# One quarter row of a tile loaded in sixteen runs of partitions, and twenty load semaphores

## The chip, the core and the metric

The kernel runs on one core of one Trainium2 chip. Data lies in device memory and is brought into the core's on-chip memory of 128 partitions by loads that the queue of SyncE (SP) issues and that 16 DMA engines carry out. Three engines compute: ScalarE (ACT), GpSimd (POOL) and VectorE (DVE). TensorE is not used. The metric is the device time of one execution in microseconds (us).

## The reference

```python
batch, seq, dim = 32, 2048, 2048
x = np.random.randn(batch, seq, dim).astype(np.float32)
mask = np.random.rand(batch, seq, dim) < 0.1
x[mask] = np.nan
...
np.nanmax(x, axis=axis).astype(np.float32)
```

The last axis is reduced: 65,536 rows of 2,048 floats, 537 MB in all, each row to its largest value that is not NaN.

## The kernel before, in words

**Layout.** The 65,536 rows are dealt to the 128 partitions, 512 rows to each. The unit of the plan is a quarter row, 512 floats, 2 KB in each partition (`Q`, line 11). `TILES` (from line 16) lists 74 tiles; an entry is (loads, pieces, reds), all in quarter rows. Most tiles are of 28 quarter rows, seven whole rows in each partition, and are brought by one load of 128 partitions x 56 KB. The first tile is of 4 quarter rows, and in the tail the tiles are cut into more and smaller loads. `GROUPS` joins tiles whose rows lie together in device memory; the 30th tile is the last of the second group.

**Three steps in a tile.** The pieces say how much each cleaning step takes, the reds how much each maximum takes.
1. ACT (`e_key`, line 270's helper) reads the upper 16 bits of a piece in a tile buffer `xt` and writes a 16-bit key to a key buffer `kt`, in which a NaN becomes a value that turns into a very low number.
2. POOL turns the key back (times -1, plus a constant, line 280's helper) and writes it over the upper 16 bits in `xt`. For pieces with a negative number ACT does this instead.
3. DVE takes the maximum along each row from `xt` (`tensor_reduce`, line 287's helper) and writes it to `acc` or `lead`.

The usual tile of 28 has pieces 7, 9, 12 and reds 16, 12. Every eighth tile or so has 9, 12, -7 and 8, 20.

**Buffers.** There are three tile buffers (`BUFS`) and three key buffers. Tile n uses buffer n mod 3, so the load of tile n waits until DVE has done its last maximum of tile n - 3 (`free`, handed to `load` as `before`).

**Order and waits.** The class `Order` keeps, for each engine, the semaphore values that it has already seen, directly or through what another engine had seen. `add` puts an explicit wait in front of the instruction for every event that is still unseen except the last one, which the instruction itself waits for. A load is put on SP's queue by `load` (line 241). It uses one of `LANES` semaphores in turn, and waits for the load that used the same one before. All loads and the six stores go through SP's queue.

**Around the change.** In the loop `for loads, pieces, reds in g` (line 346) the counter `number` is 1 for the first tile after `number += 1`. The loop over `loads` (line 352) issues one load for each entry and notes in `landed` which columns of the tile it brings. A piece's ACT step waits for every entry of `landed` that overlaps its columns (`here`). The first three loads are issued ahead and taken from the list `ahead`.

## Time and profile before

| what | before |
|---|---|
| time, median of 3 runs | 1250.41 us (1250.36 to 1250.45) |
| span of the profiled execution | 1248.8 us |
| read from device memory | 536.87 MB, 430 GB/s over the span |
| loads of 7168 KB, issue to landing | 61, median 22.6 us |

The span runs from the first to the last instruction of one profiled execution; the time of a run lies 1.6 us above it here. In the profile a row of a group names the line, the engine, the operation, the tile written and the tile read, the shape, the count, the busy time and the mean, and after a bar the idle time of the engine before these instructions with what ended it. A row of the timeline gives start, duration, engine, line, operation and, in brackets, the idle time before it. A row of stretches gives the window, its length, and the busy time of DVE, ACT and POOL with their counts, then the TensorE clock, the DMA share and GB/s. The chain of waits is read from the last instruction back, each step to what released it. Many lines of the program are helpers, so L246 is every load, L270 every ACT step, L280 every POOL step, L287 every maximum.

### The profile page before, as it was taken

Reading aid. Unit: us, or ns where it says so; the run is one execution under the profiler, and the core shown is the slowest. Engines: PE = TensorE matmul, PEld = TensorE weight load, DVE = VectorE, ACT = ScalarE, POOL = GpSimd, SP = SyncE. Lnnn points to the kernel's source line nnn. Section 1 sums busy time; section 2 is a strip of 40 time slices with the busy share of each in tenths; the row PEclk is TensorE's granted clock in tenths of the full one; section 3 lists DMA queues with packets and bytes.
Section 4 is the critical chain, followed back from the end, with each engine's and each line's share of the span. In section 5 each row is a group of like instructions: output and inputs, shape, how many; then the busy total and the mean of one; then the engine's idle time right before and its main releaser. Section 6 shows DMA issues by size and latency. Waiting matters only on the chain.

```text
span 1248.8 us, 884 instructions
## 1 busy us (share of the span) xinstructions
DVE 1110.5 (89%) x181; ACT 968.8 (78%) x280; POOL 1164.9 (93%) x238
## 2 busy tenths in 40 slices
DVE  0888989888889888898988888988888989999999
ACT  3777887778777877788777877777777779989998
POOL 2999989998999899998999899999999999999998
DMA  9999999999999999999999999999999999999998
GB/s 416 441 413 439 441 441 425 428 441 441 428 425 441 441 435 417 441 441 439 426 428 441 439 432 422 441 441 435 419 439 441 435 430 432 429 432 427 431 428 326
DMA packets 16855, 537.20 MB, mean 430 GB/s; under 512 B 2640, under 2 KB 2640, under 8 KB 4944
## 3 DMA queue, kind: packets, MB, share of 16 engines
q1 hardware_dynamic: 16848, 537.14, 99.6%
q14 instruction: 7, 0.06, 0.0%
HBM read 536.87 MB, written 0.26 MB: 430 GB/s over the span
## 4 chain that ended last, share of the span: by engine, by line
DVE 38%; DMA 36%; POOL 17%; ACT 9%; issue 1%; SPq 0%
DMA xt<-in_x_dram 36%; DVE acc L287 22%; POOL xt L280 17%; DVE lead L287 16%; ACT kt L270 8%; ACT xt L270 1%; SPq L246 0%; SPq L264 0%; SPq L255 0%
## 5 line engine op out<-in xcount | busy, mean ns | idle before, releaser
L280 POOL TENSOR_SCALAR xt<-kt 128x6144 int16<-128x6144 uint16 (+9 forms) x232 | 1163.8, 5016 | 80.5 <-ACT kt L270 67.1
L270 ACT ACTIVATE kt<-xt 128x3584 uint16<-128x3584 int16 (+10 forms) x248 | 913.0, 3720 | 271.8 <-DMA xt<-in_x_dram 250.3
L287 DVE TENSOR_REDUCE acc<-xt 128x3 f32<-128x6144 f32 (+3 forms) x119 | 896.2, 7571 | 132.9 <-POOL xt L280 125.6
L287 DVE TENSOR_REDUCE lead<-xt 128x1 f32<-128x2048 f32 (+3 forms) x59 | 212.9, 3690 | 0.5 <-POOL xt L280 0.5
L270 ACT ACTIVATE xt<-kt 128x512 int16<-128x512 uint16 (+4 forms) x30 | 57.1, 1913 | 0.6
L270 ACT ACT_TABLE_LOAD x1 | 1.3, 1283 | 3.3 <-PEq L264 3.3
L319 DVE MEMSET lead<- 128x1 f32 x1 | 0.1, 59 | 3.4 <-PEq L264 3.4
L287 DVE SCALAR_TENSOR_TENSOR acc<-acc 128x414 f32<-128x414 f32 x1 | 1.2, 1178 | 0.0
L280 POOL TENSOR_SCALAR lead<-lead 128x91 int32<-128x91 f32 x1 | 0.6, 551 | 0.1
L315 POOL TENSOR_TENSOR lead<-lead 128x91 int32<-128x91 int32 x1 | 0.4, 376 | 0.1
L526 POOL MEMSET const-float32-0.0<- 128x1 f32 x1 | 0.1, 99 | 0.2 <-issue 0.2
L270 ACT ACTIVATE lead<-lead 128x1 f32<-128x1 f32 x1 | 0.2, 203 | 0.0
L287 DVE SCALAR_TENSOR_TENSOR lead<-lead 128x7 f32<-128x7 f32 x1 | 0.2, 168 | 0.0
L526 POOL MEMSET const-bfloat16-1.0<- 128x1 bf16 x1 | 0.1, 102 | 0.0
L526 POOL MEMSET const-uint8-127<- 128x1 uint8 x1 | 0.1, 102 | 0.0
L526 POOL MEMSET const-float32-1.0<- 128x1 f32 x1 | 0.1, 99 | 0.0
## 6 DMA issues: line engine op xcount, KB each, us to landing
xt<-in_x_dram SPq DMA_DIRECT2D x61, 7168.0 KB, 22.6
xt<-in_x_dram SPq DMA_DIRECT2D x3, 4096.0 KB, 18.6
xt<-in_x_dram SPq DMA_DIRECT2D x5, 2048.0 KB, 27.5
xt<-in_x_dram SPq DMA_DIRECT2D x3, 3072.0 KB, 25.5
xt<-in_x_dram SPq DMA_DIRECT2D x2, 4352.0 KB, 16.5
xt<-in_x_dram SPq DMA_DIRECT2D x3, 2816.0 KB, 23.3
xt<-in_x_dram SPq DMA_DIRECT2D x2, 3584.0 KB, 25.2
xt<-in_x_dram SPq DMA_DIRECT2D x5, 1024.0 KB, 27.6
```

What stands on the lines that cost most here:

```text
L270: lambda: nc.scalar.activation(**kw),
L280: lambda: nc.gpsimd.tensor_scalar(**kw),
L287: return order.add("dve", nc.vector, lambda: do(**kw), deps)
L315: lambda: nc.gpsimd.tensor_tensor(out=bits, in0=bits, in1=none, op=ALU.add),
L319: e_warm = order.add("dve", nc.vector, lambda: nc.vector.memset(warm, 1.0), [])
L526: nc = _bacc.Bacc("TRN2", target_bir_lowering=False, num_devices=1)
```

## The change

The 30th tile's entry gets two loads, of 27 quarter rows and of 1. The load of 27 is issued as any other. The one quarter row behind it (`at` is not 0) is issued as sixteen loads, each of the same 512 columns but of a run of neighbouring partitions: 15, 14, 13, ... 1 of them, and 8 twice, 128 in all. Each has an entry in `landed` with the same columns, so ACT's piece over these columns waits for all of them. The number of load semaphores goes from 14 to 20. Pieces and reds of the tile are the same.

```diff
-    + [([28], [7, 9, 12], [16, 12])] * 7
+    + [([28], [7, 9, 12], [16, 12])] * 4
+    + [([27, 1], [7, 9, 12], [16, 12])]
+    + [([28], [7, 9, 12], [16, 12])] * 2
...
-LANES = 14
+LANES = 20
+
+RUNS_IN = 30
+RUNS = (15, 14, 13, 12, 11, 10, 9, 8, 8, 7, 6, 5, 4, 3, 2, 1)
...
                 if ahead:
                     e = ahead.pop(0)
+                elif number == RUNS_IN and at:
+                    p = 0
+                    for n in RUNS:
+                        e = load(
+                            xt[p : p + n, at : at + c],
+                            xg[p : p + n, base + at : base + at + c],
+                            before,
+                        )
+                        landed.append((at, at + c, e))
+                        p += n
+                    assert p == P
+                    at += c
+                    continue
                 else:
                     e = load(xt[:, at : at + c], xg[:, base + at : base + at + c], before)
```

## The prediction

> **What bounds the kernel now.** I read the page first (busy shares, DMA queues, DMA issues), then stretches of the span, the chain of waits around the 30th tile, the timeline of the tail, and last the DMA packets in narrow windows.

> ```profile
> span 1248.8 us, 884 instructions
> DVE 1110.5 (89%) x181; ACT 968.8 (78%) x280; POOL 1164.9 (93%) x238
> q1 hardware_dynamic: 16848, 537.14, 99.6%
> xt<-in_x_dram SPq DMA_DIRECT2D x61, 7168.0 KB, 22.6
> 600.00:1000.00 400.00, 357.79 (x48) 300.38 (x73) 387.09 (x71) 1.00 1.00 434
> ```

> The load queue is never empty: its packets fill 99.6% of 16 engines' span, and from 600 to 1000 us the DMA share is 1.00 at 434 GB/s. A tile of 28 quarter rows is 7168 KB = 7.34 MB; at 434 GB/s that is 16.91 us. POOL is the busiest engine (387.09 of 400 us, 97%) but not the bound. The chain through two tiles shows the period:

> ```profile
> 457.07 22.54 DMA xt<-in_x_dram
> 479.61 0.02 issue
> 479.63 3.20 ACT kt L270
> 482.83 0.07 issue
> 482.90 4.20 POOL xt L280
> ...
> 487.18 5.35 POOL xt L280
> ...
> 492.56 15.16 DVE acc L287 x2
> ...
> 507.73 22.61 DMA xt<-in_x_dram
> ```

> Three buffers, one lap of 507.73 - 457.07 = 50.66 us, or 16.89 us a tile. A load takes 22.6 us from issue to landing, 16.9 of them its own bytes: for the first 5.7 us the engines still move the tile before. That 5.7 us is the cover against a late issue.

> Around the 30th tile (tile 1 lands at about 5.5 us, so tile 30 near 5.5 + 29 x 16.91 = 496 us):

> ```profile
> 458.76 15.15 DVE L287 TENSOR_REDUCE acc<-xt 128x4 f32<-128x8192 f32 x2 [1.72 <-POOL xt L280]
> 496.54 7.12 ACT L270 ACTIVATE kt<-xt 128x3584 uint16<-128x3584 int16 x2 [4.08 <-DMA xt<-in_x_dram]
> 504.04 5.33 ACT L270 ACTIVATE kt<-xt 128x6144 uint16<-128x6144 int16 x1 [0.38 <-POOL xt L280]
> 499.81 16.73 POOL L280 TENSOR_SCALAR xt<-kt 128x3584 int16<-128x3584 uint16 x3 [0.16 <-ACT kt L270]
> ```

> DVE leaves tile 27's buffer at 473.9, the load of tile 30 is issued then, and ACT starts on it at 496.54 after 4.08 us of waiting for the DMA. POOL has 0.16 us of air in this tile.

> How far a delay reaches is decided in the tail:

> ```profile
> 1017.44 15.14 DVE L287 TENSOR_REDUCE acc<-xt 128x4 f32<-128x8192 f32 x2 [0.54 <-POOL xt L280]
> 1020.97 10.54 ACT L270 ACTIVATE kt<-xt 128x6144 uint16<-128x6144 int16 x2 [4.19 <-DMA xt<-in_x_dram]
> 1040.75 206.37 DVE L287 TENSOR_REDUCE lead<-xt 128x3 f32<-128x6144 f32 x58 [0.49 <-POOL xt L280]
> 1247.16 0.17 DVE L287 SCALAR_TENSOR_TENSOR lead<-lead 128x7 f32<-128x7 f32 x1
> ```

> From 1040.75 DVE never stops: 206.37 us in one piece to the end. So the end is the landing at 1020.95 plus a fixed rest, and what counts is by how much the change moves that landing. A later one is passed on in full; an earlier one finds 0.54 + 0.49 = 1.03 us of DVE idle time to take out.

> Last, a landing is not one moment. Each engine closes its share with a tiny packet (under 512 B). The strip has 40 slices, of 20 ns and of 25 ns:

> ```profile
> DMA  0000000000000009099909000900099990000000
> DMA packets 26, 0.75 MB, mean 932 GB/s; under 512 B 13, under 2 KB 13, under 8 KB 13
> ...
> DMA  0000000000000009000000990000000000000000
> DMA packets 6, 0.17 MB, mean 172 GB/s; under 512 B 3, under 2 KB 3, under 8 KB 3
> ```

> These are the windows 1019.2 to 1020 and 1020 to 1021 us: 13 engines close from 1019.5 to 1019.9, three at 1020.4 and 1020.6. The last is 1.1 us behind the first, and the tile waits for it. The trace gives no engine's name, so which three these are is unknown.

> **The change, part by part.** The other 73 tiles keep their loads. In the 30th, 27 quarter rows come in one load and the 28th in sixteen, for 15, 14, ... 1 partitions with 8 twice: 16 transfers more, the same bytes.

> How a transfer is cut, and what small ones cost:

> ```profile
> DMA packets 142, 7.28 MB, mean 455 GB/s; under 512 B 15, under 2 KB 15, under 8 KB 15
> ...
> 1236.00:1241.00 5.00, 5.00 (x4) 5.00 (x7) 4.53 (x4) 1.00 1.03 412
> ```

> The first row is the window 497 to 513: 127 data packets in 7.28 MB, 57 KB each, one partition's row; with 16 closers a load, 8 rows an engine. The second is a stretch of the tail where the loads are of 256 and 512 KB: 412 GB/s. A quarter row over 128 partitions (262144 B) takes 0.604 us at 434 and 0.636 at 412 GB/s. So a 2 KB packet is 0.0755 us (0.604 / 8), 0.080 with its share of a closer, and a closer at most 0.032.

> *Engines.* A run of n rows is n packets, so for n below 16 at most n engines work on it. If the first always gets its first row, engine 0 gets a packet of all 16 runs, engine 15 none, the one between in steps: 16 to 9 for engines 0 to 7, then 7 to 0. Engine 0: 16 packets with 16 closers, 16 x 0.080 = 1.28 to 16 x 0.1075 = 1.72 us, less 0.604: **+0.68 to +1.12 us**; I take +0.8, nearer the row of small loads. Engine 15: -0.6. The lag stays, since every engine works its queue without a gap. The landing moves by the latest engine alone. If that is a low one, it goes from 1.1 to 1.9 (+0.8); if all three late ones are high, they fall to 0.5 to 0.7 while engine 0, with a lag of 0 to 0.4 so far, comes to 0.8 to 1.2 (-0.3 to +0.1). Mixed, +0.3 to +0.8. I take **+0.6**. Bounds: rows dealt evenly, 16 more closers spread out, about 0; all 128 on one engine, 128 x 0.080 - 0.6 = +9.6.

> [...]

> *SP.* It issues 17 instead of 1:

> ```profile
> L246 SPq DMA_DIRECT2D xt<-in_x_dram x3: 374/421/424, 1.0 to 1.9; - x3
> L246 SPq DMA_DIRECT2D xt<-in_x_dram x23: 328/1417/8181, 1185.8 to 1230.1; - x23
> ```

> At 0.42 us each (first row) and a gap of 0.05, 16 x 0.47 = 7.5 us more, from 474.3 to 481.8. The bytes ahead of the runs last until 496, and SP's next work, tile 31's load, is due at 490.8. Cost nothing; were that cover gone, 7.5 us. Twenty semaphores instead of 14: a load now waits for the load 20 back, and with 17 in one tile that lies before tile 30 for all of them and has landed. No wait is added on SP.

> *ACT, POOL, DVE.* ACT's first two pieces (7 and 9 quarters) need only the load of 27, which lands 0.6 us sooner; the third must wait for 17 semaphores, 16 of them new. Queued behind is its 5.33 us key step, and POOL's last piece waits for that. The runs land about 1 to 2 us after the big load, the third piece starts 7.5 us after the first, so all have landed; the new waits cost 0.02 to 0.07 us each (the gaps that the chain above calls issue), 0.3 to 1.1 us, against 0.38 us in which ACT waits for POOL there. POOL loses up to 0.7 us once, makes up about 0.16 a tile, and the buffer comes free later by as much, against a cover of 5.7 us. Nothing at the end.

> **Sum.** Span 1248.8 + 0.6 = 1249.4; the median of the runs lies 1.6 us over the span (1250.41), so **1251.0 us**.

> **Rivals.**

> *Relief.* The late engines are all high ones: -0.3 to 0, 1250.2 us. For: three stand apart from thirteen. Against: nothing tells their number.

> *Neighbours collide.* A full load sends each engine to its own eight rows; a run sends up to 15 engines at once to neighbouring rows. If four neighbours share one way into the memory at one engine's pace, each of the thirteen runs of 4 or more lasts 4 packets: 13 x 0.32 + 6 x 0.08 = 4.6, less 0.6, +4.0 us without overlap, and about +2.4 if two in five of it overlap with the next run or next tile: **1252.8 us**, slower by 0.2%. It decides from four on; sharing by two overlaps away. For: each engine moves 434 / 16 = 27.1 GB/s and not more with long rows, as behind a fixed port. Against: no row shows two engines in neighbouring rows. [...]

> *The queue is full.* In the tail an issue lasted up to 8.18 us (the row of 23, median 1.42): SP was held where many loads were queued. If it holds at about ten loads whatever their size, nine runs enter, and seven and tile 31's load wait until the 27 have landed: 8 x 0.42 = 3.4 us of issue, less 0.5 us of queued bytes, +2.9, less about 0.2 because the late engines catch up: **1253.1 us**. Against: a run brings one data packet an engine, not eight; counted in packets the queue is nearly empty.

> *One engine gets the odd runs.* Where n shares no factor with 16 on few engines: from 86 packets on one engine, 86 x 0.080 - 0.6 = +6.3, to all 128, +9.6: 1257 to 1260 us.

> *Out of step is quicker.* Staggered engines might hinder each other less; 0.2% would need 2.5 / 31 = 0.08 us off each tile to 1020 us. Against: 434 GB/s at every stretch without a wait.

> **How the numbers follow.** 0.2% is 2.5 us, about what a measurement of this kernel can tell from no change. Chances: forecast 0.43 (1250.4 to 1251.2), relief 0.11, neighbours 0.20 (0.08 within 0.2%, 0.12 over), full queue 0.10, one engine 0.12, quicker out of step 0.04. Faster 0.04; same 0.43 + 0.11 + 0.08 = 0.62; slower 0.12 + 0.10 + 0.12 = 0.34. Range 1249.9 to 1254.5: relief at its best, neighbours without overlap at the top; it leaves out the one-engine case and the quicker one, 0.16, and their like.

> **What would show it.** Right: closers of tile 31 spread by up to 2 us, ACT's start on the landing of 1020.95 later by 0.6, period still 16.91, DVE's last stretch still 206.4. Neighbours: the runs' packets take several times 0.08 us, and most engines are late together. Full queue: an SP issue of many us at 478 and a gap in the DMA strip at 497. One engine: one closer of tile 31 late by over 6 us. I am wrong if the landing at 1020.95 moves by over 1 us.

## The result, and the profile after

The changed kernel takes 1253.29 us (median of nine executions) against 1250.41 us: a ratio of 1.0022, 95% interval 1.0014 to 1.0031, so 2.9 us slower. Three more executions of it, and none of the kernel before, took 1341 us and are left out; in the one execution of this sort that was profiled, of the kernel e2 below, the loads ran at about 385 GB/s from the runs to the end, so e2's packets are not used here.

The page of the kernel after, span and busy shares, the load queue and the loads of whole tiles:

```profile
span 1251.3 us, 908 instructions
...
DVE 1110.6 (89%) x181; ACT 968.7 (77%) x280; POOL 1164.4 (93%) x238
...
q1 hardware_dynamic: 17104, 537.14, 99.6%
...
xt<-in_x_dram SPq DMA_DIRECT2D x60, 7168.0 KB, 22.7
xt<-in_x_dram SPq DMA_DIRECT2D x3, 4096.0 KB, 20.6
```

The engines compute what they computed, the bytes are the same 537.14 MB. There are 17104 - 16848 = 256 more packets: 128 of 2 KB and 128 more closers. So each row of a run has a closer of its own. A whole load, too, has 16 closers for 16 engines, eight rows each (of tile 31 here, from 513.13 to 515.45 us, by the packet records); read that way, a run of n rows went to n engines. Which engine got which row is not in the trace.

A stretch of the kernel after, with the columns as before:

```profile
600.00:1000.00 400.00, 358.73 (x48) 300.49 (x73) 387.04 (x71) 1.00 1.00 434
```

From 600 to 1000 us the rate is 434 GB/s, the number of before. The loss is a single step, and ACT's timeline of the kernel after shows where it is:

```profile
479.99 7.12 ACT L275 ACTIVATE kt<-xt 128x3584 uint16<-128x3584 int16 x2 [4.07 <-DMA xt<-in_x_dram]
...
497.12 7.12 ACT L275 ACTIVATE kt<-xt 128x3584 uint16<-128x3584 int16 x2 [4.31 <-DMA xt<-in_x_dram]
...
504.62 5.32 ACT L275 ACTIVATE kt<-xt 128x6144 uint16<-128x6144 int16 x1 [0.38 <-POOL xt L285]
515.86 3.19 ACT L275 ACTIVATE kt<-xt 128x3584 uint16<-128x3584 int16 x1 [5.91 <-DMA xt<-in_x_dram]
```

The last of these rows is ACT's start on tile 31. In the kernel before, it came here:

```profile
513.44 3.19 ACT L270 ACTIVATE kt<-xt 128x3584 uint16<-128x3584 int16 x1 [4.07 <-DMA xt<-in_x_dram]
```

Tile 29 starts 0.36 us later than before (479.99 against 479.63; ahead of the change, so not of its making), tile 30 0.58, tile 31 2.42. The runs and the tile behind them cost 2.42 - 0.36 = 2.06 us: 0.22 up to the landing of the load of 27, which should even have come 0.6 us sooner, and 1.84 more up to the landing of tile 31, where ACT waits 5.91 us for the DMA instead of 4.07. In the third row above ACT's last piece of tile 30 still waits 0.38 us for POOL: the sixteen more semaphores to wait for cost nothing there.

The tail of the kernel after passes it on, as the rows of before said:

```profile
1023.30 10.54 ACT L275 ACTIVATE kt<-xt 128x6144 uint16<-128x6144 int16 x2 [4.21 <-DMA xt<-in_x_dram]
...
1043.07 206.52 DVE L292 TENSOR_REDUCE lead<-xt 128x3 f32<-128x6144 f32 x58 [0.48 <-POOL xt L285]
1249.62 0.17 DVE L292 SCALAR_TENSOR_TENSOR lead<-lead 128x7 f32<-128x7 f32 x1
```

The landing at 1020.95 moved by 2.33 us, DVE's last stretch is 206.5 us, the last step 2.46 us later. The span of this execution grew by 2.5 us; the medians, over many executions, differ by 2.9.

### The profile page after: what moved, and what is told of

Read it like the earlier page. It is cut to its first block, busy times and chain, and to the rows that moved or that the text cites. A ratio compares the mean times of both kernels' runs of the same rounds, so it can differ in the third digit from the quotient of the medians.

```text
span 1251.3 us, 908 instructions
## 1 busy us (share of the span) xinstructions
DVE 1110.6 (89%) x181; ACT 968.7 (77%) x280; POOL 1164.4 (93%) x238
## 3 DMA queue, kind: packets, MB, share of 16 engines
q1 hardware_dynamic: 17104, 537.14, 99.6%
## 4 chain that ended last, share of the span: by engine, by line
DMA 37%; DVE 34%; POOL 18%; ACT 10%; issue 1%; SPq 0%
DMA xt<-in_x_dram 37%; DVE acc L292 22%; POOL xt L285 18%; DVE lead L292 12%; ACT kt L275 9%; ACT xt L275 1%; SPq L251 0%; SPq L269 0%; SPq L260 0%
## 6 DMA issues: line engine op xcount, KB each, us to landing
xt<-in_x_dram SPq DMA_DIRECT2D x60, 7168.0 KB, 22.7
```

## The experiments

The theories after the result: (1) the uneven count alone, as forecast; (2) engines collide where they write into the chip's memory; (3) all packets slow while small and large ones run side by side, or where many closers do. The trace records start, length and size of each DMA packet; the table below is worked out from these records. Undisturbed, a packet of 2 KB lasts 84 ns, one of a whole tile's row (57344 B) 2.116 us. "Lost" is what the packets around the quarter row lasted over their undisturbed length, summed over 16 engines; each figure comes from one execution. The kernel after and e8, the same runs in two tiles, differ by 1.1 engine-us, so differences of that size are not told apart. The kernel e12, whose last runs come apart from the others, is not in the table.

```
kernel           median us  how the 28th quarter row comes      2 KB packets:    57 KB packets begun  lost,
                                                                mean ns, >95 ns  meanwhile, mean us   engine-us
after            1253.29    16 runs of 15..1 neighbours         107   68 of 128  3.12                 19.6
e1_plain         1250.54    one load of 128                      84    0 of 128  2.12                  0.0
e3_apart8        1252.77    16 x 8, every 4th                    96   29 of 128  3.09                 18.0
e4_near16        1251.68    8 x 16 neighbours                   109   55 of 128  2.86                 16.1
e5_apart16       1251.51    8 x 16, every 8th                    94   38 of 128  2.67                 10.4
e6_mem_apart     1251.87    reads every 8th, writes neighbours  110   50 of 128  2.80                 16.1
e7_chip_apart    1251.67    reads neighbours, writes every 8th   95   40 of 128  2.71                 11.7
e8_tile29        1253.16    as after, a tile earlier            106   62 of 128  3.06                 18.5
e9_own_half      1250.93    8 x 8, every 4th, rows 0-63          84    0 of  64  2.16                  0.6
e10_other_half   1251.85    8 x 8, every 4th, rows 64-127       104   31 of  64  2.95                 15.5
e11_near_half    1251.57    8 x 8 neighbours, rows 0-63          98   21 of  64  2.82                 12.7
```

**e1: the split and the semaphores alone.**

```diff
-                    p = 0
-                    for n in RUNS:
...
+                    e = load(
+                        xt[:, at : at + c],
+                        xg[:, base + at : base + at + c],
+                        before,
+                    )
+                    landed.append((at, at + c, e))
```

> The quarter row behind the 27 comes as one load of 128 partitions; twenty semaphores stay. All theories: the split itself and the number of semaphores cost nothing, 1250.3 to 1250.6 us, and the landing of tile 31 moves by under 0.1 us. If the time rises by over 0.5 us, the second load or the semaphores bear part of the loss.

Measured 1250.54 us, ratio 1.0001 (0.9991 to 1.0010). ACT's start on tile 31 in this kernel:

```profile
513.61 7.13 ACT L275 ACTIVATE kt<-xt 128x3584 uint16<-128x3584 int16 x2 [4.22 <-DMA xt<-in_x_dram]
```

That is 0.17 us later than before, and 0.12 of it was there at tile 29 already (479.75 against 479.63). Every small packet lasts 84 ns, with the next tile's packets beside them at 2.12 us. So neither the second load nor the number of semaphores costs anything that shows, and small packets beside large ones, cut as any load is cut, don't slow.

**e2 and e3: sixteen runs of 8, neighbours or every fourth.**

```diff
-                    for n in RUNS:
+                    for p in range(0, P, 8):                                             # e2
+                    for p in [a + b for a in range(0, P, 32) for b in range(4)]:         # e3
...
-                            xt[p : p + n, at : at + c],
+                            xt[p : p + 8, at : at + c],                                  # e2
+                            xt[p : p + 29 : 4, at : at + c],                             # e3
...
+                            xg[p : p + 8, base + at : base + at + c],                    # e2
+                            xg[p : p + 29 : 4, base + at : base + at + c],               # e3
```

A comment behind a line names the kernels that have it.

> Sixteen runs of 8 neighbouring partitions: the first eight engines get 16 packets each, the others none. Uneven count alone: the landing of tile 31 0.8 us later, 1250.9 to 1251.3 us, with every small packet at about 0.085 us and the next tile's packets at 2.116 us. Neighbours collide: more, 1252 to 1254 us. Everything slows while small and large packets run side by side: also 1252 to 1254 us.

> Sixteen runs of 8 again, the same packets for each engine as in the kernel with 8 neighbours, but every fourth partition instead of neighbours. Uneven count alone: the same as that kernel, 1250.9 to 1251.3 us. Neighbours collide: at least 1 us less than the kernel with 8 neighbours. Everything slows beside large packets, whatever the partitions: within 0.4 us of the kernel with 8 neighbours and 1252 us or more.

e2 took 1253.55 us (median of eight executions; ratio 1.0024, 95% interval 1.0014 to 1.0034), e3 1252.77 (1.0019, 1.0010 to 1.0029). Both lose far more than the 0.5 to 0.9 us of an uneven count, and neighbours 0.8 us more than every fourth, under the 1 us expected of a collision of neighbours and over the 0.4 us of the third theory: not decided. e3's packets say more. Its runs 1 to 8 go to partitions 0 to 63, 9 to 16 to 64 to 127, and the first 91 packets to start all last 84 ns; the first slow one starts 1.29 us after the first small packet, by an estimate about 0.6 us after the first engines came to the second half (8 packets at 86 ns are 0.69 us). In the kernel after, and in the other kernels of this table that slow, that is 0.56 to 0.80 us after the first small packet.

**e4 to e7: eight runs of 16, 8 packets for each engine by the count of closers.** Read so, no engine gets more than another here. e4 takes neighbours, e5 every eighth, e6 and e7 one in the memory and the other on the chip.

```diff
+                    for p in range(0, P, 16):            # e4
+                    for p in range(8):                   # e5, e6, e7
...
+                            xt[p : p + 16, at : at + c],                                  # e4
+                            xt[p : p + 121 : 8, at : at + c],                             # e5, e7
+                            xt[16 * p : 16 * p + 16, at : at + c],                        # e6
...
+                            xg[p : p + 16, base + at : base + at + c],                    # e4
+                            xg[p : p + 121 : 8, base + at : base + at + c],               # e5, e6
+                            xg[16 * p : 16 * p + 16, base + at : base + at + c],          # e7
```

> Eight runs of 16 neighbouring partitions: every engine gets 8 packets, so none is ahead of the others. Uneven count alone: 1250.4 to 1250.7 us. Neighbours collide: 1251.5 us or more, and small packets well over 0.085 us. Everything slows beside large packets: little, as the small ones of all engines run at one time, 1250.5 to 1251.2 us.

> Eight runs of 16 as in the kernel with 16 neighbours, but every eighth partition, in the memory and on the chip. If neighbours on the chip collide: clearly under the 1251.68 us of that kernel, 1250.5 to 1251.2 us. If the closers of eight small loads, or small packets as such, cost the 1.2 us: 1251.5 to 1251.9 us again.

> Reads every eighth row in the memory and writes 16 neighbouring partitions on the chip; the quarter row lands in other partitions than it belongs to, so this part of the output is another row's. Collision at the way into the chip's memory: 1251.5 to 1251.9 us, like 16 neighbours in both. Collision at the reads: like every eighth in both, 1250.5 to 1251.2 us.

> The other way round: reads 16 neighbouring rows in the memory and writes every eighth partition; the quarter row lands in other partitions than it belongs to. Collision at the way into the chip's memory: 1250.5 to 1251.2 us. Collision at the reads: 1251.5 to 1251.9 us.

e4 is 1.2 us slower than before (1.0010, 1.0001 to 1.0019) with an even count, if the closers are read rightly: that part has nothing to do with the count. e5 at 1251.51 (0.9999 to 1.0018), e6 at 1251.87 (1.0002 to 1.0021) and e7 at 1251.67 (1.0000 to 1.0019) lie too close together for the times to tell. By their windows, e5 and e7 missed the collision on the chip: e5 fell where closers or small packets as such were expected, e7 where the reads were. The packets do tell: with neighbours on the chip 16.1 engine-us are lost whichever rows are read (e4, e6), with every eighth 10.4 and 11.7 (e5, e7). So most of what these packets show goes with the writes; with the order of the reads it changes by 0 and 1.3, about what two traces of the same runs differ by. But spreading by eight takes about a third of the loss away and not all, and these four leave open whether the eight closers an engine have a share in it.

**e8: the change one tile earlier.**

```diff
-    + [([28], [7, 9, 12], [16, 12])] * 4
+    + [([28], [7, 9, 12], [16, 12])] * 3
     + [([27, 1], [7, 9, 12], [16, 12])]
-    + [([28], [7, 9, 12], [16, 12])] * 2
+    + [([28], [7, 9, 12], [16, 12])] * 3
...
-RUNS_IN = 30
+RUNS_IN = 29
```

> The change in the 29th tile instead of the 30th, so the tile behind it lies in the same group of rows. If the loss is bound to the runs themselves: 1253 to 1253.7 us as before. If it comes of reading the first tile of a new group beside the end of the old one: 1250.9 to 1251.5 us, what the uneven count alone would make.

1253.16 us (1.0023, 1.0013 to 1.0033): the first tile of a group of rows has no part in it.

**e9 to e11: half a quarter row, 64 packets of 2 KB in eight runs of 8.** All three leave the other 64 partitions of the quarter row out.

```diff
+                    for p in [a + b for a in (0, 32) for b in range(4)]:       # e9,  xt[p : p + 29 : 4, ...]
+                    for p in [a + b for a in (64, 96) for b in range(4)]:      # e10, xt[p : p + 29 : 4, ...]
+                    for p in range(0, 64, 8):                                  # e11, xt[p : p + 8, ...]
```

> The quarter row of partitions 0 to 63 alone, in eight runs of 8 that take every fourth partition, 0 4 8 to 28 and so on; that of partitions 64 to 127 is not loaded. Each of the first eight engines gets 8 packets and 8 closers. In the kernel with every fourth partition of all 128, the small packets kept 0.084 us for the first half of the runs and slowed in the second. If each of the eight engines here has a way into the chip's memory to itself: all small packets at 0.084 us, next tile's packets at 2.116 us, 1250.2 to 1250.6 us. If many closers slow the loads: small packets over 0.1 us, 1251 us or more. [...]

> As the kernel with its own half, but for partitions 64 to 127, in the same eight runs of 8 with every fourth partition; that of 0 to 63 is not loaded. [...] Two engines share a way in: small packets over 0.1 us from about 0.6 us after the first, next tile's first packets over 2.116 us, time 0.4 to 1 us over that kernel. Closers: the same as that kernel.

> Partitions 0 to 63 again, in eight runs of 8 neighbours; 64 to 127 are not loaded. The same eight engines with 8 packets and 8 closers each. Neighbours share a way in: slow small packets and slow packets of the next tile, 0.5 to 1.2 us over the kernel with its own half. Closers, or reading and writing small packets as such: the same as that kernel.

1250.93 us for e9 (ratio 1.0004, 0.9995 to 1.0014), 0.3 us above the window expected; 1251.85 for e10 (1.0011, 1.0001 to 1.0021) and 1251.57 for e11 (1.0010, 1.0000 to 1.0019), both inside theirs. ACT's start on tile 31 in e9 and in e10:

```profile
513.80 7.12 ACT L275 ACTIVATE kt<-xt 128x3584 uint16<-128x3584 int16 x2 [4.29 <-DMA xt<-in_x_dram]
```

```profile
514.75 7.12 ACT L275 ACTIVATE kt<-xt 128x3584 uint16<-128x3584 int16 x2 [5.13 <-DMA xt<-in_x_dram]
```

Counted from ACT's start on tile 29 (479.86 in e9, 479.83 in e10), this is 33.94 and 34.92 us, against 33.81 in the kernel before: the runs of e9 delay tile 31 by 0.13 us, those of e10 by 1.11. Rows of e9, e10 and e11 in this order, the packets that started from 495.7 to 497.7 us:

```profile
DMA packets 64, 0.85 MB, mean 424 GB/s; under 512 B 28, under 2 KB 28, under 8 KB 50
```

```profile
DMA packets 66, 0.40 MB, mean 200 GB/s; under 512 B 33, under 2 KB 33, under 8 KB 60
```

```profile
DMA packets 67, 0.40 MB, mean 201 GB/s; under 512 B 33, under 2 KB 33, under 8 KB 61
```

Bytes are counted where a packet starts, so a window this short isn't a rate, but the three stand side by side: 22 to 28 packets of 2 KB in each (under 8 KB less under 2 KB), and e9's engines start 0.85 MB where the other two start 0.40. In e9 all 64 small packets last 84 ns. So what makes the loss of e10 and e11 is not the number of closers, not small packets as such, not the length or number of the runs, which are alike in all three, but which partitions a run takes. e11 reads the same rows as e9 in another order, e10 the other half; that the reads bear the loss is unlikely after e4 to e7, where their order changed little, but no run reads e10's rows and writes e9's partitions. That each engine has partitions of its own, which the runs of e9 keep to and those of e10 and e11 don't, was the author's estimate; it is not shown, since the trace names no engine. What is shown are the losses: 0.6 engine-us for every fourth partition of 0 to 63 (e9), 15.5 for every fourth of 64 to 127 (e10), 12.7 for neighbours of 0 to 63 (e11).

**e12: the change with 14 semaphores.**

```diff
-LANES = 20
+LANES = 14
```

> The change with 14 load semaphores instead of 20. The 14th run then waits for the load of 27, and behind it on SP stand two more runs and the load of tile 31. If the wait is what the twenty avoid: SP held until 497 us, then three or four issues of 0.4 us, the queue empty for 1 to 3 us, 1254 to 1256 us. If the semaphores make no difference: 1253 to 1253.7 us.

1253.93 us, ratio 1.0027 (1.0017 to 1.0038). The waits of SP and ACT's start on tile 31 in this kernel:

```profile
SPq L251 <- DMA xt<-in_x_dram: 17.4, 2, 16.6
```

```profile
517.18 3.19 ACT L275 ACTIVATE kt<-xt 128x3584 uint16<-128x3584 int16 x1 [7.72 <-DMA xt<-in_x_dram]
```

SP is held 16.6 us by the load of 27, as expected, and tile 31 comes at 517.18, another 1.3 us after the kernel with twenty. The time is just under the range expected. The twenty semaphores avoid this wait; what it is worth at the end is not settled, since the medians are 0.6 us apart and their intervals overlap.

## Why the prediction was right or wrong

The time lies inside the range stated, but the likeliest case did not happen: the landing at 1020.95 moved by 2.33 us, and the prediction called itself wrong beyond 1 us. That the range held is owed to the rival at its upper end, not to the mechanism of the forecast. What held: the loads bound the kernel, the landing at 1020.95 decides, and DVE's last piece passes a delay on in full (2.33 us at the landing, 2.46 at the end).

**The step that failed** is the engines' one, where the price of a small packet was taken from loads of 128 partitions and the +0.6 us worked out from the count alone. No run shows one engine with a packet of every run, which the +0.8 us takes for granted; what the packet records show is that the first sixteen packets of tile 31 start over 2.73 us (495.16 to 497.90), against 0.87 in the kernel before. The price of the count alone holds as far as it can be worked out: undisturbed, packet and closer follow each other every 86 ns (e9), so sixteen on one engine come to 16 x 0.086 - 0.604 = +0.77 us against the +0.8 taken; no run shows an uneven count without slow packets. But the price of a packet did not hold in these runs: 107 ns on average, and the next tile's packets 3.12 us instead of 2.12. The forecast put nothing on the next tile's packets, and there lies most of the loss. The step of 2.06 us less at most 0.77 leaves 1.3 us or more to the slow packets, and e4, with 8 packets for each engine as its closers are read, shows 1.2 us.

**The rival that came true in part** is the colliding neighbours, forecast at 1252.8 us. No run shows four partitions that share one way into the memory, from which it is added up. What the runs show is that neighbours do slow, by 16.1 engine-us (e4) and 12.7 (e11), but that runs without neighbours can slow as well: every fourth partition of 64 to 127 by 15.5 (e10). And it was priced as slow small packets alone, four packet times (0.32 us) for each run, while the small packets took 107 ns on average and the larger part of the loss, 15.7 of 19.6 engine-us, is on the large packets of the next tile. That its 1252.8 us came near the 1253.29 measured is therefore luck.

**The other steps.** *Sixteen more issues on SP:* forecast 7.5 us, all hidden. Its row in the kernel after:

```profile
L251 SPq DMA_DIRECT2D xt<-in_x_dram x17: 252/296/485, 474.3 to 480.1; - x17
```

The last starts at 480.1, 5.8 us after the first, and none takes over 0.485 us. The load of tile 31, issued at 491.2 while the 17 of tile 30 are still under way, takes 0.36 us: SP is not held with 18 loads under way, so the rival of the full queue falls. *One engine gets the odd runs* falls with the 256 packets. *Relief* did not show: the landing moved later. *Out of step is quicker* did not show either: the rate from 600 to 1000 us stays at 434 GB/s. *ACT's new waits* cost nothing that the rows show. *The lag stays*, forecast as constant: ACT is 2.42 us late at tile 31 and 2.33 at 1023.30. *Closers of tile 31* were to spread over up to 2 us; windows of the kernel after, 512.5 to 514 and 514 to 516 us, show ten and six of the 16:

```profile
DMA  0090000000009000909990900990000000009000
DMA packets 24, 0.80 MB, mean 535 GB/s; under 512 B 10, under 2 KB 10, under 8 KB 10
...
DMA  0090009000000090000009909099090990000009
DMA packets 22, 0.92 MB, mean 459 GB/s; under 512 B 6, under 2 KB 6, under 8 KB 6
```

The strips hold other packets too; by the packet records of the closers, the 16 land within 2.3 us.

## What to carry to other kernels

A quarter row cut off by columns, over all 128 partitions, loses nothing that shows (e1: 84 ns for every small packet, 1250.54 us). Cut into runs of partitions, it depends on which partitions a run takes: here one whole quarter row, 256 KB of 537 MB, cost 1.0 to 3.1 us (after, e2 to e8), while half of one in runs of every fourth partition of 0 to 63 lost next to nothing in its packets (e9, 0.6 engine-us). Here the stream of loads is the bound (99.6% of 16 engines' span), and one late engine was enough: in the kernel before, 13 of 16 engines had closed the tile by 1019.9, the last came at 1020.6, and ACT started at 1020.97. The delay is carried to the end: the 2.06 us at tile 31 were still 1.97 at 1023.30. A price taken from a row holds for the way in which that row's transfers were cut: the 0.080 us for a small packet with its share of a closer came from loads of 128 partitions, and in the runs of the kernel after the packet alone took 0.107.

## What the runs showed of the hardware

Nor is it settled why e5 and e7 still lose 10 to 12 engine-us, though they write every eighth partition and no neighbours.
